# Four element-wise steps of an FFN's tile pair moved from GpSimd to VectorE

## The chip, the cores and the metric

The kernel runs on one core of one Trainium2 chip. The time is the device time of one execution in microseconds; three runs of the kernel before gave 2213.86, 2218.98 and 2221.95 us. An engine is named as in the profile: PE (TensorE), DVE (VectorE), ACT (ScalarE), POOL (GpSimd) and SP (SyncE, which only issues the weight loads here).

## The reference

One inference step of two layers of a decoder, over 512 prompt tokens and 8 x 4 sample tokens, which the kernel keeps side by side as 544 columns. Each layer does

```python
h = h + 0.5 * swiglu(rmsnorm(h, g_ffn1), w1_a, w3_a, w2_a)     # FFN a
h = h + concat(ssd(...), window_attention(...)) @ w_out         # mixing
h = h + 0.5 * swiglu(rmsnorm(h, g_ffn2), w1_b, w3_b, w2_b)     # FFN b
h = h + sigmoid(rmsnorm(h, g_ple) @ w_ple_gate) * (p @ w_ple_proj)

def swiglu(x, w1, w3, w2):
    return (silu(x @ w1) * (x @ w3)) @ w2
```

with a model width of 1024 and an FFN width of 2752, in float32. The change touches the four FFNs (two layers, a and b) alone.

## The kernel before, in words

**Precision.** Every float32 operand of a matmul is split into a high part (a copy rounded to fp32r) and a low part (what is left), and a product is the sum of three: high x high, high x low and low x high. For weights that is `split`: ACT makes the copy (line 100), DVE the difference (line 101). A weight unit is 4 x 128 rows by 128 columns of a weight, 128 x 512 in SBUF. All weight loads are issued by SP, in the order of the program, each into a buffer that an earlier unit must have left.

**An FFN.** The state `h` lies as 8 tiles of 128 x 544. An FFN has a head (`plain`: five plain products against all of `h`, two gated tiles and the remainder of 64 columns, and `block_sums`, which forms four sums of blocks of the normed input) and then 19 *pairs*, in groups of 3, 4, 4, 4 and 4. A pair computes one 128-column tile of x @ w1 and of x @ w3 together, from seven half-products instead of eight, as in Strassen's scheme. With a11, a12 the two halves (in k) of the w1 tile and a21, a22 those of w3, the weight sums are

- q1 = a21 + a22 (line 347, POOL)
- a21 = a21 + a11 (line 348, POOL)
- a11 = a11 + q1 (line 349, DVE)
- a12 = a12 + a11 (line 354, DVE)

each followed by its split; splits of sums are named `q` in the profile (`qh`, `ql`), splits of plain weights `w` (`wh`, `wl`). PE then does seven products of 12 matmuls (line 363) into four PSUM banks, three of which are used twice; after each product DVE reads the bank (lines 373 to 383; the first, line 371, is ACT's) and adds it to `v`, `c2` or `t`, so that a bank's second product waits for the first one's reader. `t` becomes x @ w1 with its columns times Rb (1/rms of the token): the first half in line 379 with the bank's read, the second in line 383 and then line 384 (POOL). `gated` (lines 249 to 254) makes silu: tanh of t/2 on ACT (251), (tanh + 1) * t on DVE (252), times Rb on POOL (253). Line 386 (DVE) multiplies by x @ w3, and `keep` splits the result for the last product (ACT 262, DVE 263).

**Down tiles.** Behind each pair stand two or three of the eight tiles of the last product of the group before (`last(m)`): in group 1, 16 matmuls each, 2, 3 and 3 of them behind its three pairs; in group 2, 18 matmuls each, two behind each pair; in groups 3 to 5, 24 each, two behind each pair. Their matmuls are those of line 128, their split is line 101 again, and DVE adds each half into `h` (line 334). So PE has 84 + 32 or 84 + 48 matmuls per pair in group 1, 120 in group 2, and 132 in groups 3 to 5.

**What sets the order.** The program names tiles and operations; a scheduler with its own cost figures gives each engine its queue, and each engine works through its own in order. A step that is put on another engine can therefore shift other steps on both. Buffers set how far the weights run ahead: six for `raw` (a21, a22 and the down tiles), four for `ra` (a11, a12), two for q1, six for the splits of plain weights and four for those of sums.

Of the kernel before, what the change touches and what calls it, by code (L numbers as in the profile page):

```python
# [12 lines left out]
ALU = mybir.AluOpType  # L13
# [26 lines left out]
def hymba_step(ctx: ExitStack, tc: tile.TileContext, I, O):  # L40
    nc = tc.nc
    V, A, G, PE = nc.vector, nc.scalar, nc.gpsimd, nc.tensor
# [7 lines left out]
    def bank():  # L50
        return psp.tile([128, 512], F32, tag="ps", name="ps")
# [28 lines left out]
    Rb = base.tile([128, N], F32, tag="Rb", name="Rb")  # L80
# [10 lines left out]
    def raw_unit(loads, pool=wp, tag="raw", bufs=None):  # L91
        raw = pool.tile([128, KU, 128], F32, tag=tag, name=tag, bufs=bufs)
        for dst, src in loads:
            nc.sync.dma_start(out=dst(raw), in_=src)
        return raw

    def split(raw, n=KU, pool=wp, tag="w", bufs=None):
        wh = pool.tile([128, KU, 128], F32R, tag=tag + "h", name=tag + "h", bufs=bufs)
        wl = pool.tile([128, KU, 128], F32R, tag=tag + "l", name=tag + "l", bufs=bufs)
        A.copy(wh[:, 0:n, :], raw[:, 0:n, :])  # L100
        V.tensor_sub(wl[:, 0:n, :], raw[:, 0:n, :], wh[:, 0:n, :].bitcast(F32))  # L101
        return wh, wl
# [12 lines left out]
    def terms3(p, k, xh, xl):  # L115
        wh, wl = p[k // KU]
        k %= KU
        return [(wh[:, k, :], xh), (wh[:, k, :], xl), (wl[:, k, :], xh)]
# [20 lines left out]
    HALF = (slice(0, HN), slice(HN, N))  # L139
# [97 lines left out]
    def ffn(g, w1, w3, w2, begun=None):  # L237
# [5 lines left out]
        with tc.tile_pool(name="ffn", bufs=2, reuse_waits="tile") as fp:  # L243
# [5 lines left out]
            def gated(t1, np_=128):  # L249
                th = fp.tile([128, N], F32, tag="th", name="th")  # L250
                A.activation(th[0:np_, :], t1[0:np_, :], AF.Tanh, scale=0.5)
                V.scalar_tensor_tensor(th[0:np_, :], th[0:np_, :], 1.0, t1[0:np_, :], op0=ALU.add, op1=ALU.mult)  # L252
                G.tensor_tensor(th[0:np_, :], th[0:np_, :], Rb[0:np_, :], op=ALU.mult)  # L253
                return th

            def act(ps1, np_=128):
                t1 = fp.tile([128, N], F32, tag="t1", name="t1")
                evac_r(t1, ps1, np_)
                return gated(t1, np_)

            def keep(U, i, u):
                A.copy(U[:, 0, i, :], u)  # L262
                V.tensor_sub(U[:, 1, i, :], u, U[:, 0, i, :].bitcast(F32))
# [73 lines left out]
            def pair(j, sums, U, i):  # L337
                def unit(w, k, pool, tag, bufs):
                    src = w[k * 512:(k + 1) * 512, j * 128:(j + 1) * 128].rearrange("(k p) m -> p k m", p=128)
                    return raw_unit([(lambda t: t, src)], pool, tag, bufs)  # L340

                a11 = unit(w1, 0, fp, "ra", 4)
                a21, a22 = unit(w3, 0, wp, "raw", None), unit(w3, 1, wp, "raw", None)
                a12 = unit(w1, 1, fp, "ra", 4)
                f11 = split(a11)
                q1 = fp.tile([128, KU, 128], F32, tag="q1", name="q1")
                G.tensor_tensor(q1, a21, a22, op=ALU.add)  # L347
                G.tensor_tensor(a21, a21, a11, op=ALU.add)
                V.tensor_tensor(a11, a11, q1, op=ALU.add)
                g2 = split(a11, KU, fp, "q", 4)  # L350
                g3 = split(a21, KU, fp, "q", 4)
                g1 = split(q1, KU, fp, "q", 4)
                f12 = split(a12)
                V.tensor_tensor(a12, a12, a11, op=ALU.add)
                f22 = split(a22)
                g4 = split(a12, KU, fp, "q", 4)
                t2, t3, t1, t4 = sums
                x11, x21, x22 = ((XH[:, k:k + KU, c:c + HN], XL[:, k:k + KU, c:c + HN]) for k, c in ((0, 0), (KU, 0), (KU, HN)))

                def prod(ps, f, x, start):  # L360
                    for k in range(KU):
                        for n, (lhsT, rhs) in enumerate(terms3([f], k, x[0][:, k, :], x[1][:, k, :])):
                            PE.matmul(ps[:, 0:HN], lhsT, rhs, start=start and k == 0 and n == 0, stop=k == KU - 1 and n == 2,  # L363
                                      skip_group_check=not start)

                pa, pb, pc, pd = bank(), bank(), bank(), bank()
                v = fp.tile([128, 2, HN], F32, tag="v", name="v")
                t = fp.tile([128, N], F32, tag="t1", name="t")
                c2 = fp.tile([128, N], F32, tag="c2", name="c2")
                prod(pa, f11, x11, True)  # L370
                A.copy(v[:, 0, :], pa[:, 0:HN])  # L371
                prod(pb, g2, t2, True)
                V.tensor_sub(v[:, 0, :], v[:, 0, :], pb[:, 0:HN])  # L373
                prod(pc, g3, t3, True)
                V.tensor_sub(v[:, 1, :], v[:, 0, :], pc[:, 0:HN])  # L375
                prod(pd, g1, t1, True)
                V.tensor_tensor(c2[:, HALF[1]], v[:, 1, :], pd[:, 0:HN], op=ALU.add)  # L377
                prod(pa, f12, x21, False)
                V.tensor_tensor(t[:, HALF[0]], pa[:, 0:HN], Rb[:, HALF[0]], op=ALU.mult)
                prod(pc, f22, t4, False)  # L380
                V.tensor_sub(c2[:, HALF[0]], v[:, 0, :], pc[:, 0:HN])
                prod(pd, g4, x22, False)
                V.tensor_tensor(t[:, HALF[1]], v[:, 0, :], pd[:, 0:HN], op=ALU.add)  # L383
                G.tensor_tensor(t[:, HALF[1]], t[:, HALF[1]], Rb[:, HALF[1]], op=ALU.mult)  # L384
                th = gated(t)
                V.tensor_tensor(c2, c2, th, op=ALU.mult)  # L386
                keep(U, i, c2)
# [8 lines left out]
            for j0, n in ((2, PH - 1), (5, PH), (9, PH), (13, PH), (17, PH)):  # L396
                U = uset()
                for i in range(n):
                    ms = range(KD * i // n, KD * (i + 1) // n)
                    pair(j0 + i, sums, U, i)  # L400
                    for m in ms:
                        last(m)
                last = lambda m, U=U, j0=j0, n=n: down(j0, n, U, m)
# [884 lines left out]
```

## Time and profile before

| | |
|---|---|
| runs | 2213.86, 2218.98, 2221.95 us (median 2218.98) |
| profiled execution | 2219.62 us, its span 2217.8 us, mean granted clock 0.98 |
| line 347 on POOL | 76 instructions of 128x512, 107.1 us, mean 1409 ns |
| line 348 on POOL | 76 of 128x512, 120.3 us, mean 1583 ns |
| line 384 on POOL | 76 of 128x272, 64.7 us, mean 852 ns |
| line 253 on POOL | 84 of 128x544, 120.9 us, mean 1439 ns, and 4 of 64x544, 8.2 us |
| line 354 on DVE | 76 of 128x512, 95.1 us, mean 1251 ns |
| line 101 on DVE, sums in `ra` | 152 of 128x512, 166.6 us, mean 1096 ns |

Times in the profile are of one execution and in us, unless marked ns. A row such as `L349 TENSOR_TENSOR ra<-ra,q 128x512` is line 349's instruction, out<-in with its shape (partitions x elements). A bracket at the end of a row is the idle time of its engine just before it and what ended that. Rows of one engine can overlap by some tens of ns.

### The profile page before, as it was taken

The numbers are of one execution on the slowest core, as the hardware profiler recorded it, in microseconds if no ns is written. First come the engines' busy times: TensorE is split into PE (matmuls) and PEld (weight loads), VectorE is DVE, ScalarE is ACT, GpSimd is POOL, SyncE is SP. The second block draws the span as 40 slices with busy tenths as digits, with TensorE's granted clock in tenths as the row PEclk, the third lists the DMA queues.
The fourth block names the chain that finished last, engine by engine and source line by source line (L and its number), as shares of the span: only waits on it lengthen the run. The fifth ranks groups of instructions, "written<-read, shape, count | busy, mean of one in ns | idle before, by whom it ended". The sixth has DMA issues, their size and how long they took to land.

```text
span 2217.8 us, 43407 instructions
## 1 busy us (share of the span) xinstructions
PE 2135.3 (96%) x16754; PEld 2088.9 (94%) x16754; DVE 1799.6 (81%) x3250; ACT 953.8 (43%) x1768; POOL 667.4 (30%) x589
## 2 busy tenths in 40 slices
PE   7999999999999999999998999999999998999999
PEld 7989999988899999999988999999898998999998
DVE  7889897589867999886578999874987689998864
ACT  5434443444445344444453344443443453444443
POOL 3323322233522332322123332322334223333220
PEclk9999999999999999999999999999998999999999
DMA  6333332313241433322323333332133423333222
GB/s 178 92 104 91 105 92 76 81 48 89 69 125 47 111 86 105 96 82 84 90 73 102 93 91 101 86 82 70 51 86 87 114 68 92 96 92 105 73 84 72
DMA packets 401210, 197.88 MB, mean 89 GB/s; under 512 B 40270, under 2 KB 400358, under 8 KB 401004
## 3 DMA queue, kind: packets, MB, share of 16 engines
q1 hardware_dynamic: 399420, 194.93, 32.2%
q8 instruction: 132, 2.16, 0.4%
q14 instruction: 74, 0.61, 0.1%
q10 hardware_dynamic: 1584, 0.18, 0.1%
HBM read 187.56 MB, written 9.53 MB: 89 GB/s over the span
## 4 chain that ended last, share of the span: by engine, by line
PE 49%; DVE 10%; issue 3%; ACT 1%; POOL 1%; DMA 1%; SPq 0%; ACTq 0%; DVEq 0%; POOLq 0%
PE ps L128 26%; PE ps L363 20%; DVE wl L101 3%; DVE ql L101 1%; DVE h L334 1%; POOL th L253 1%; DMA raw<-in_w_b 1%; DVE c L386 1%; ACT qh L100 0%; PE ps L910 0%; DVE T L280 0%; ACT U L262 0%; DVE CV L664 0%; DVE v L375 0%; DVE v L373 0%
## 5 line engine op out<-in xcount | busy, mean ns | idle before, releaser
L128 PE MATMUL ps<-U,wh 128*128 128x272 f32 x2752 | 524.8, 289 | 0.0
L100 ACT CAST wh<-raw 128x512 fp32r<-128x512 f32 (+2 forms) x460 | 272.8, 597 | 482.3 <-PE ps L128 255.8
L128 PEld LDWEIGHTS ps<-U,wh 128*128 128x128 f32 x2752 | 433.7, 189 | 0.1
L101 DVE TENSOR_TENSOR wl<-raw,wh 128x512 fp32r<-128x512 f32 (+2 forms) x460 | 345.7, 756 | 84.6 <-ACT wh L100 76.3
L128 PE MATMUL ps<-U,wl 128*128 128x272 f32 x1408 | 400.0, 287 | 0.0
L128 PE MATMUL ps<-XH,wh 128*128 128x272 f32 x1312 | 385.8, 296 | 9.1 <-ACT wk L552 5.3
L128 PE MATMUL ps<-XL,wh 128*128 128x272 f32 x1312 | 380.0, 291 | 1.8 <-DVE XL L158 1.6
L128 PE MATMUL ps<-XH,wl 128*128 128x272 f32 x1280 | 371.4, 291 | 0.0
L128 PEld LDWEIGHTS ps<-U,wl 128*128 128x128 f32 x1408 | 264.3, 188 | 0.0
L128 PEld LDWEIGHTS ps<-XH,wh 128*128 128x128 f32 x1312 | 249.2, 190 | 14.0 <-ACT wk L552 5.7
L128 PEld LDWEIGHTS ps<-XL,wh 128*128 128x128 f32 x1312 | 250.2, 191 | 3.7 <-DVE XL L158 3.3
L128 PEld LDWEIGHTS ps<-XH,wl 128*128 128x128 f32 x1280 | 243.6, 190 | 0.0
L363 PE MATMUL ps<-T,qh 128*128 128x272 f32 x1216 | 236.0, 291 | 4.1 <-DVE T L280 2.9
L384 POOL TENSOR_TENSOR t<-t,Rb 128x272 f32<-128x272 f32 x76 | 64.7, 852 | 475.8 <-DVE t L383 423.8
L347 POOL TENSOR_TENSOR q<-raw 128x512 f32<-128x512 f32 x76 | 107.1, 1409 | 314.2 <-DMA raw<-in_w_b 141.1
L363 PEld LDWEIGHTS ps<-T,qh 128*128 128x128 f32 x1216 | 193.4, 190 | 5.2 <-DVE T L280 3.6
L363 PE MATMUL ps<-XH,wh 128*128 128x272 f32 x608 | 177.6, 292 | 14.5 <-ACT v L371 9.8
L253 POOL TENSOR_TENSOR th<-th,Rb 128x544 f32<-128x544 f32 (+1 forms) x88 | 129.1, 1467 | 179.6 <-DVE th L252 173.5
L363 PE MATMUL ps<-XL,qh 128*128 128x272 f32 x608 | 178.5, 294 | 1.3 <-DVE XL L280 1.3
L363 PE MATMUL ps<-T,ql 128*128 128x272 f32 x608 | 176.9, 292 | 0.9 <-DVE ql L101 0.7
L363 PE MATMUL ps<-XH,qh 128*128 128x272 f32 x608 | 177.1, 291 | 0.6 <-DVE c L377 0.6
L363 PE MATMUL ps<-XH,ql 128*128 128x272 f32 x608 | 177.6, 292 | 0.0
(389 smaller groups left out, 4977.8 us busy)
## 6 DMA issues: line engine op xcount, KB each, us to landing
raw<-in_w_a SPq DMA_DIRECT2D x156, 256.0 KB
raw<-in_w_b SPq DMA_DIRECT2D x156, 256.0 KB
ra<-in_w_a SPq DMA_DIRECT2D x76, 256.0 KB
ra<-in_w_b SPq DMA_DIRECT2D x76, 256.0 KB
raw<-in_w_in SPq DMA_DIRECT2D x60, 256.0 KB
raw<-in_w_ple_gate SPq DMA_DIRECT2D x32, 256.0 KB
raw<-in_w_in SPq DMA_DIRECT2D x32, 128.0 KB
raw<-in_w_out SPq DMA_DIRECT2D x32, 128.0 KB
```

The lines of the kernel that those rows point to most:

```text
L100: A.copy(wh[:, 0:n, :], raw[:, 0:n, :])
L101: V.tensor_sub(wl[:, 0:n, :], raw[:, 0:n, :], wh[:, 0:n, :].bitcast(F32))
L128: PE.matmul(ps[a][:, 0:HN], lhsT, rhs[:, a * HN:(a + 1) * HN], start=gi == 0 and i == 0, stop=gi == n - 1 and i == len(terms) - 1)
L253: G.tensor_tensor(th[0:np_, :], th[0:np_, :], Rb[0:np_, :], op=ALU.mult)
L334: V.scalar_tensor_tensor(h[:, m, HALF[a]], ps[a][:, 0:HN], f, h[:, m, HALF[a]], op0=ALU.mult, op1=ALU.add)
L347: G.tensor_tensor(q1, a21, a22, op=ALU.add)
L363: PE.matmul(ps[:, 0:HN], lhsT, rhs, start=start and k == 0 and n == 0, stop=k == KU - 1 and n == 2, skip_group_check=not start)
L384: G.tensor_tensor(t[:, HALF[1]], t[:, HALF[1]], Rb[:, HALF[1]], op=ALU.mult)
L386: V.tensor_tensor(c2, c2, th, op=ALU.mult)
```

## The change

The four operations of a pair that were POOL's, lines 253, 347, 348 and 384, are given to DVE, operands and results being the same. Line 253 stands in `gated`, so the three gated tiles of the head go with it.

```diff
@@ -250,7 +250,7 @@
                 A.activation(th[0:np_, :], t1[0:np_, :], AF.Tanh, scale=0.5)
                 V.scalar_tensor_tensor(th[0:np_, :], th[0:np_, :], 1.0, t1[0:np_, :], op0=ALU.add, op1=ALU.mult)
-                G.tensor_tensor(th[0:np_, :], th[0:np_, :], Rb[0:np_, :], op=ALU.mult)
+                V.tensor_tensor(th[0:np_, :], th[0:np_, :], Rb[0:np_, :], op=ALU.mult)
                 return th
@@ -344,8 +344,8 @@
                 q1 = fp.tile([128, KU, 128], F32, tag="q1", name="q1")
-                G.tensor_tensor(q1, a21, a22, op=ALU.add)
-                G.tensor_tensor(a21, a21, a11, op=ALU.add)
+                V.tensor_tensor(q1, a21, a22, op=ALU.add)
+                V.tensor_tensor(a21, a21, a11, op=ALU.add)
                 V.tensor_tensor(a11, a11, q1, op=ALU.add)
@@ -381,7 +381,7 @@
                 V.tensor_tensor(t[:, HALF[1]], v[:, 0, :], pd[:, 0:HN], op=ALU.add)
-                G.tensor_tensor(t[:, HALF[1]], t[:, HALF[1]], Rb[:, HALF[1]], op=ALU.mult)
+                V.tensor_tensor(t[:, HALF[1]], t[:, HALF[1]], Rb[:, HALF[1]], op=ALU.mult)
                 th = gated(t)
                 V.tensor_tensor(c2, c2, th, op=ALU.mult)
```

The queues of DVE are in another order by it. In group 2, DVE's queue of the kernel before, around the first evacuations of one pair (`v_9764`); `ra_9922`, `ra_9928`, `raw_9924` and `q1_9934` belong to the next pair's weights, `ra_9725` is the pair's own a12:

```order
L263 TENSOR_TENSOR U_9312<-c2_9563,U_9312 128x544
L334 SCALAR_TENSOR_TENSOR h_70<-ps_9698,h_70 128x272
L101 TENSOR_TENSOR wl_9931<-ra_9922,wh_9930 128x512
L349 TENSOR_TENSOR ra_9922<-ra_9922,q1_9934 128x512
L101 TENSOR_TENSOR wl_9951<-ra_9928,wh_9950 128x512
L373 TENSOR_TENSOR v_9764<-v_9764,ps_9761 128x272
L354 TENSOR_TENSOR ra_9928<-ra_9928,ra_9922 128x512
L101 TENSOR_TENSOR ql_9939<-ra_9922,qh_9938 128x512
L375 TENSOR_TENSOR v_9764<-v_9764,ps_9762 128x272
```

and the same place after the change:

```order
L263 TENSOR_TENSOR U_9312<-c2_9563,U_9312 128x544
L354 TENSOR_TENSOR ra_9725<-ra_9725,ra_9719 128x512
L101 TENSOR_TENSOR wl_9897<-raw_9894,wh_9896 128x384
L373 TENSOR_TENSOR v_9764<-v_9764,ps_9761 128x272
L101 TENSOR_TENSOR ql_9757<-ra_9725,qh_9756 128x512
L101 TENSOR_TENSOR wl_9931<-ra_9922,wh_9930 128x512
L375 TENSOR_TENSOR v_9764<-v_9764,ps_9762 128x272
L347 TENSOR_TENSOR q1_9934<-raw_9924,raw_9926 128x512
L377 TENSOR_TENSOR c2_9766<-v_9764,ps_9763 128x272
L348 TENSOR_TENSOR raw_9924<-raw_9924,ra_9922 128x512
```

The next pair's first sums now stand behind L375 of this pair instead of ahead of it, and the last sum of this pair's own weights (L354 on `ra_9725`) and its split have moved in between its evacuations.

In a pair of groups 3 to 5, DVE's queue before, from one pair's L386 on (`v_11032` is the next pair, `wl_11171` a split of a down tile):

```order
L386 TENSOR_TENSOR c2_10818<-c2_10818,th_10911 128x544
L334 SCALAR_TENSOR_TENSOR h_70<-ps_10925,h_70 128x272
L101 TENSOR_TENSOR wl_11171<-raw_11168,wh_11170 128x512
L263 TENSOR_TENSOR U_10125<-c2_10818,U_10125 128x544
L334 SCALAR_TENSOR_TENSOR h_70<-ps_10958,h_70 128x272
L334 SCALAR_TENSOR_TENSOR h_70<-ps_10959,h_70 128x272
L101 TENSOR_TENSOR wl_11211<-ra_11202,wh_11210 128x512
L349 TENSOR_TENSOR ra_11202<-ra_11202,q1_11214 128x512
L101 TENSOR_TENSOR wl_11231<-ra_11208,wh_11230 128x512
L354 TENSOR_TENSOR ra_11208<-ra_11208,ra_11202 128x512
L373 TENSOR_TENSOR v_11032<-v_11032,ps_11029 128x272
L101 TENSOR_TENSOR ql_11219<-ra_11202,qh_11218 128x512
```

and after the change:

```order
L386 TENSOR_TENSOR c2_10818<-c2_10818,th_10911 128x544
L334 SCALAR_TENSOR_TENSOR h_70<-ps_10958,h_70 128x272
L101 TENSOR_TENSOR wl_11171<-raw_11168,wh_11170 128x512
L263 TENSOR_TENSOR U_10125<-c2_10818,U_10125 128x544
L334 SCALAR_TENSOR_TENSOR h_70<-ps_10959,h_70 128x272
L101 TENSOR_TENSOR wl_11211<-ra_11202,wh_11210 128x512
L349 TENSOR_TENSOR ra_11202<-ra_11202,q1_11214 128x512
L101 TENSOR_TENSOR wl_11231<-ra_11208,wh_11230 128x512
L347 TENSOR_TENSOR q1_11429<-raw_11419,raw_11421 128x512
L373 TENSOR_TENSOR v_11032<-v_11032,ps_11029 128x272
L101 TENSOR_TENSOR ql_11219<-ra_11202,qh_11218 128x512
L354 TENSOR_TENSOR ra_11208<-ra_11208,ra_11202 128x512
```

The sum L347 of a later pair (`q1_11429`) now stands in DVE's queue ahead of L373 and the evacuations behind it, five instructions behind the split `wl_11171`, whose end frees the buffer that the last of L347's two loads goes into.

## The prediction

> **What bounds the kernel now.** I read the busy line first, then the windows, the chain of waits, the starts of one instruction that every pair has (line 386), and last the rows of one pair on VectorE and GpSimd.
>
> ```profile
> PE 2135.3 (96%) x16754; PEld 2088.9 (94%) x16754; DVE 1799.6 (81%) x3250; ACT 953.8 (43%) x1768; POOL 667.4 (30%) x589
> ```
>
> TensorE (PE) is busy for 2135.3 of the span's 2217.8 us, so at most 82.5 us can be had without touching matmuls. VectorE (DVE) at 81% looks like the last engine to give more work. That is an average; by stages it reads otherwise (columns: window, length, busy of PE, weight load, DVE, ACT, POOL, then the granted clock):
>
> ```profile
> 1180.00:1285.00 105.00, 94.31 (x719) 92.78 (x718) 97.82 (x153) 40.84 (x76) 35.05 (x26) 0.97 0.34 95
> 1285.00:1468.00 183.00, 183.00 (x1459) 183.00 (x1459) 158.04 (x261) 77.14 (x129) 51.24 (x40) 1.00 0.33 92
> 1212.00:1220.00 8.00, 5.47 (x24) 5.48 (x25) 5.89 (x11) 0.97 (x2) 1.57 (x1) 0.57 0.32 87
> ```
>
> These lie in the third FFN. In the pair groups 3 to 5 (second row) PE never rests and DVE has 25 us free. In groups 1 and 2 (first row) PE rests 10.7 us of 105, and DVE is busy for 93%. PE waits there for DVE:
>
> ```profile
> PE ps L363 <- DVE v L375: 29.9, 21, 4.3
> 1214.53 0.82 PE L363 MATMUL ps<-T,wh 128*128 128x272 f32 x2 [4.34 <-DVE v L375]
> ```
>
> A product that writes a bank which L375 must first read stands still. After the longest such stall the clock row shows 0.57: 24 matmuls take 5.47 us, 0.228 each, against the full rate in the chain of waits:
>
> ```profile
> 834.78 6.01 PE ps L128 x48
> 840.78 10.57 PE ps L363 x84
> ```
>
> That is 0.1255 us per matmul. From one L386 to the next, PE has 84 matmuls of products and the down tiles of the pair between. In group 1 these are 116, 132 and 132 matmuls up to the first pair of group 2; in group 2 four times 120 (two down tiles of 18). At full rate, group 1 needs 380 x 0.1255 = 47.7 us and group 2 480 x 0.1255 = 60.2 us per FFN. The starts of the 1st, 4th and 8th pair's L386, for the four FFNs:
>
> ```profile
> 73.65 0.72 DVE L386 TENSOR_TENSOR c<-c,th 128x544 f32<-128x544 f32 x1 [0.77 <-POOL th L253]
> 127.92 0.72 DVE L386 TENSOR_TENSOR c<-c,th 128x544 f32<-128x544 f32 x1 [1.26 <-POOL th L253]
> 194.52 0.73 DVE L386 TENSOR_TENSOR c<-c,th 128x544 f32<-128x544 f32 x1 [1.14 <-POOL th L253]
> 719.03 0.72 DVE L386 TENSOR_TENSOR c<-c,th 128x544 f32<-128x544 f32 x1 [0.78 <-POOL th L253]
> 774.28 0.71 DVE L386 TENSOR_TENSOR c<-c,th 128x544 f32<-128x544 f32 x1
> 839.05 0.73 DVE L386 TENSOR_TENSOR c<-c,th 128x544 f32<-128x544 f32 x1 [1.14 <-POOL th L253]
> 1167.96 0.73 DVE L386 TENSOR_TENSOR c<-c,th 128x544 f32<-128x544 f32 x1 [0.78 <-POOL th L253]
> 1224.87 0.71 DVE L386 TENSOR_TENSOR c<-c,th 128x544 f32<-128x544 f32 x1
> 1289.65 0.73 DVE L386 TENSOR_TENSOR c<-c,th 128x544 f32<-128x544 f32 x1 [1.14 <-POOL th L253]
> 1814.00 0.72 DVE L386 TENSOR_TENSOR c<-c,th 128x544 f32<-128x544 f32 x1 [0.78 <-POOL th L253]
> 1870.72 0.71 DVE L386 TENSOR_TENSOR c<-c,th 128x544 f32<-128x544 f32 x1
> 1935.51 0.73 DVE L386 TENSOR_TENSOR c<-c,th 128x544 f32<-128x544 f32 x1 [1.14 <-POOL th L253]
> ```
>
> Group 1 takes 54.3, 55.3, 56.9 and 56.7 us: 32.4 us over PE's need in all. Group 2 takes 66.6, 64.8, 64.8 and 64.8: 20.0 us over. So 52 of the 82.5 us lie where DVE sets the pace, and the pair groups 3 to 5 have nothing to give.
>
> **Why DVE is slow there.** One pair of group 2, on DVE and then on POOL (start, duration):
>
> ```profile
> 789.28 1.58 DVE L101 TENSOR_TENSOR wl<-raw,wh 128x384 fp32r<-128x384 f32 x1
> 790.78 0.71 DVE L386 TENSOR_TENSOR c<-c,th 128x544 f32<-128x544 f32 x1
> 791.42 0.43 DVE L334 SCALAR_TENSOR_TENSOR h<-ps,h 128x272 f32<-128x272 f32 x1
> ...
> 793.92 1.78 DVE L349 TENSOR_TENSOR ra<-ra,q 128x512 f32<-128x512 f32 x1
> 795.63 1.79 DVE L101 TENSOR_TENSOR wl<-ra,wh 128x512 fp32r<-128x512 f32 x1
> 797.34 0.43 DVE L373 TENSOR_TENSOR v<-v,ps 128x272 f32<-128x272 f32 x1
> 797.69 0.68 DVE L354 TENSOR_TENSOR ra<-ra 128x512 f32<-128x512 f32 x1
> 798.29 0.68 DVE L101 TENSOR_TENSOR ql<-ra,qh 128x512 fp32r<-128x512 f32 x1
> 798.89 0.42 DVE L375 TENSOR_TENSOR v<-v,ps 128x272 f32<-128x272 f32 x1
> 799.24 0.68 DVE L101 TENSOR_TENSOR ql<-raw,qh 128x512 fp32r<-128x512 f32 x1
> ...
> 803.26 1.27 DVE L101 TENSOR_TENSOR ql<-ra,qh 128x512 fp32r<-128x512 f32 x1
> ```
>
> ```profile
> 789.08 1.36 POOL L253 TENSOR_TENSOR th<-th,Rb 128x544 f32<-128x544 f32 x1 [1.61 <-DVE th L252]
> 793.87 1.29 POOL L347 TENSOR_TENSOR q<-raw 128x512 f32<-128x512 f32 x1 [3.42 <-DMA raw<-in_w_b]
> 795.23 1.63 POOL L348 TENSOR_TENSOR raw<-raw,ra 128x512 f32<-128x512 f32 x1
> 803.21 0.78 POOL L384 TENSOR_TENSOR t<-t,Rb 128x272 f32<-128x272 f32 x1 [6.35 <-DVE t L383]
> ```
>
> Each of the four GpSimd instructions falls on a DVE instruction with two operands in SBUF, and that one ends 0.4 to 0.6 us after GpSimd's does: 1.58, 1.78, 1.79 and 1.27 us, where the same forms undisturbed take about 0.55 (estimated from 128x512's 0.68), 0.68, 0.68 and 0.68. So one pair pays 1.0 + 1.1 + 1.1 + 0.6 = 3.8 us on DVE for GpSimd's help.
>
> **The change, part by part.** All four operations become DVE instructions. Start to start (rows overlap by some 0.07 us) a 128x512 costs 0.60 (797.69 to 798.29), a 128x272 0.35 (798.89 to 799.24) and a 128x544 0.64 (790.78 to 791.42). L347 and L348 add 1.20, L384 0.35, L253 0.64: 2.19 us per pair, 76 pairs, and 12 more L253 in the four heads. GpSimd then has no work left in a pair, so the 3.8 us should go: a net 1.6 us less on DVE per pair, in the groups where DVE is the bound.
>
> *Group 2.* A pair takes (66.6 + 3 x 64.8) / 16 = 16.31 us now. 16.31 - 3.8 + 2.19 = 14.7, plus about 0.3 because L252, L253 and L386 now follow each other on one engine with a result in between: 15.0, against PE's 15.06. DVE falls just under PE. With the two so close I leave 0.2 us per pair: gain 20.0 - 16 x 0.2, about 17. Least: the gap between the two rows closes only half (10). Most: 20.
>
> *Group 1.* The same net gain per pair, on intervals of 18.1 to 19 us. By DVE's work alone they would fall to PE's need. But the first pairs have no stock: their weights are prepared by DVE while it still finishes the block sums, and the longest stall (4.34 us, with the half clock behind it) lies here. I keep some 2.5 us per FFN: gain 32.4 - 10, about 22. Least 0, most 32.
>
> *Groups 3 to 5.* DVE is busy 158.04 of 183 us, or 14.3 of a pair's 132 x 0.1255 = 16.57. With 2.19 more and no relief at all that is 16.5, still under PE; with relief near 14. I cost them at nothing. PE's own matmuls hide it. The cover is thin only if DVE must wait (first rival).
>
> *Waits on POOL, and the heads.*
>
> ```profile
> DVE c L386 <- POOL th L253: 64.8, 58, 1.8
> DVE u L292 <- POOL th L253: 8.3, 7, 1.3
> ```
>
> The 64.8 us of waits at L386 go too, but most lie in groups 3 to 5 and are worth nothing. In the heads 8.3 us of DVE waits at L292 stand ahead of the block sums that PE's first pair needs; I take half, 4 (0 to 8).
>
> Sum: 17 + 22 + 4 = 43 us off the profiled run's 2219.62 (span 2217.8 and 1.8 around it; 0.6 above the median of the runs): **2177 us**, 1.9% less. The ends of the terms give 10 to 60 us, so 2160 to 2210.
>
> **The rivals.**
>
> *A: only half comes back.* The scheduler has put DVE's queue in a new order in groups 1 and 2: weight splits that ran a pair ahead now stand among the evacuations of the pair before. If L375 stands as late as it does now in group 1, the 32.4 us stay and only group 2's 17 is had: about 2202. For it: group 1's stalls depend on order, not only on sums.
>
> *B: nothing.* The saved 3.8 us reappear as the added 2.19 us and as waits inside the longer DVE chain L383, L384, (tanh on ACT), L252, L253, L386: 2217. Against it: the rows above show the overlap four times in one pair.
>
> *C, slower: L347 holds DVE's queue.* On POOL this sum waited for its weights with nothing behind it but L348. On DVE the evacuations that PE needs (L373, L375) stand behind it. The rows of a pair in group 3:
>
> ```profile
> 922.88 0.68 DVE L101 TENSOR_TENSOR wl<-raw,wh 128x512 fp32r<-128x512 f32 x1
> 923.59 0.37 SPq L94 DMA_DIRECT2D raw<-in_w_b  x1
> 926.54 1.43 POOL L347 TENSOR_TENSOR q<-raw 128x512 f32<-128x512 f32 x1 [4.69 <-DMA raw<-in_w_b]
> ```
>
> A split frees the buffer, the load is issued, and 2.95 us later L347 starts. In the new order five DVE instructions (0.64 + 0.35 + 0.60 + 0.60 + 0.60 = 2.8 us) stand between that split and L347, so DVE waits some 0.2 us, inside the 16.57 - 14.3 = 2.3 us (some 1.5 when its small gaps are counted) that a pair leaves. If the load came x us late, the 48 pairs of groups 3 to 5 would each lose x - 1.5: it eats the whole gain at x = 2.4, and a load taking twice as long (x = 3) gives 2177 + 72 = 2249.
>
> *D, slower: the long rows are not GpSimd's doing.* If the 1.6 us rows stayed long without GpSimd, each pair of groups 1 and 2 would just get 2.19 us more: 28 x 2.19 = 61, so 2281. The rows speak against it: the four long ones are those, and only those, that run under a GpSimd row, and each ends just after it. The Trainium skill, Perfetto Trace Analysis, section Optimizing Scalar/DVE Operations, says that when VectorE is saturated, giving some of its work to ScalarE or even GpSimd may make sense, which for groups 1 and 2 is this rival; it adds that VectorE and GpSimd share an SBUF read port, so that moving work between those two might not help. By its first half the sum would be 2281, by its second it stays at 2177; the rows of this pair agree with the second (1.78 us against 0.68).
>
> **How the numbers follow.** Forecast 0.62, A 0.20, B 0.08, C 0.07, D 0.03. A measurement of this kernel can tell about 0.5% from no change, here 11 us: faster means under 2208, slower over 2230. The forecast and A lie below: 0.82. B with the low edge of C gives 0.09 within, C and D 0.09 slower. Range: the lower end is the 60 us bound less 2 (2158); the upper takes A whole and stops at 2208, leaving B, C, D outside. The likeliest case's own range is 2160 to 2192.
>
> **What would show it.** Right: POOL has no row of these four lines left; L101, L349 and L354 fall to 0.68 everywhere; the L386 starts in group 2 lie 15.1 to 15.4 us apart, in group 1 within 3 us per FFN of 47.7; PE's wait on L375 falls below 10 us. Wrong in group 1: these rows shrink, yet PE still waits for L375 with the low clock behind it. Wrong by C: DVE's idle time before L347 behind a DMA, and L386 intervals over 16.6 in groups 3 to 5.

## The result and the profile after

The changed kernel takes 2154.53 us (median of 2149.38 to 2156.97) against 2218.49 us for the kernel before, measured beside it. The ratio is 0.9715, with a 95% interval from 0.9696 to 0.9734: 64 us less, where 42 were forecast (2177 us) and 2158 us was the low end of the range. The profiled execution took 2153.38 us, its span 2151.6.

The page's busy line of the changed kernel, and two of its windows, the four pairs of group 2 and ten pairs of groups 3 to 5 in the second FFN:

```profile
PE 2112.0 (98%) x16754; PEld 2071.7 (96%) x16754; DVE 1803.1 (84%) x3566; ACT 953.4 (44%) x1768; POOL 247.3 (11%) x273
732.35:792.61 60.26, 60.26 (x482) 60.26 (x481) 58.95 (x117) 27.15 (x49) 0.00 (x0) 1.00 0.41 113
809.18:974.91 165.73, 165.73 (x1322) 165.73 (x1321) 151.37 (x282) 72.02 (x121) 0.00 (x0) 1.00 0.33 91
```

The same group 2 in the kernel before:

```profile
754.21:823.18 68.97, 62.85 (x482) 61.98 (x481) 66.06 (x102) 27.42 (x51) 22.56 (x17) 0.98 0.35 97
```

Three things stand in these rows. VectorE has 316 instructions more and is busy for 1803.1 us against 1799.6: what it was given, it no longer spends standing still. TensorE now never rests in group 2 (60.26 of 60.26 us, and 480 matmuls x 0.1255 are 60.24), and VectorE does its larger share with 58.95 us of busy time instead of 66.06. (Of the 8.71 us by which this stretch is shorter, 7.11 are VectorE's busy time and 1.60 its idle time.) And TensorE's own busy time fell by 23.3 us with the same 16754 matmuls, while the mean granted clock rose from 0.98 to 0.989: a matmul at the low clock counts as busy for longer (0.228 us against 0.1255 in the prediction's rows).

VectorE's groups of the changed kernel (line, form, count, busy us, mean ns, then its idle time before them), and the group in which GpSimd is now busy longest, which was fourth before, behind lines 253, 348 and 347:

```profile
L101 DVE TENSOR_TENSOR ql<-ra,qh 128x512 fp32r<-128x512 f32 x152 | 104.3, 686 | 5.3 <-ACT qh L100 0.4
L253 DVE TENSOR_TENSOR th<-th,Rb 128x544 f32<-128x544 f32 x84 | 60.6, 721 | 1.4
L347 DVE TENSOR_TENSOR q<-raw 128x512 f32<-128x512 f32 x76 | 52.3, 688 | 6.1 <-DMA raw<-in_w_a 4.6 <-DMA raw<-in_w_b 0.9
L384 DVE TENSOR_TENSOR t<-t,Rb 128x272 f32<-128x272 f32 x76 | 33.1, 435 | 0.2
L354 DVE TENSOR_TENSOR ra<-ra 128x512 f32<-128x512 f32 x76 | 52.0, 684 | 0.1
```

```profile
L167 POOL TENSOR_TENSOR acc<-acc,sq 128x544 f32<-128x544 f32 x49 | 68.1, 1389 | 1496.5 <-ACT sq L166 1496.3
```

The splits `ql<-ra` fell from a mean of 1096 ns to 686, L354 from 1251 to 684. L347 waits 5.5 us for its loads in the whole program.

To see where the time went, the start of each pair's first product on TensorE serves better than the starts of L386 that the prediction used, because L386 itself lay behind GpSimd. Between these starts TensorE has the same number of matmuls in both kernels. The two measures cut the time at other places: the products of pair 4 belong to group 2 here, but to "group 1" between the 1st and the 4th L386. The table is worked out from them, in us against the profiled kernel before, summed over the four FFNs ("rest" is all from the last pair of one FFN to the first of the next, with the program's two ends, which moves by up to 6 us from kernel to kernel):

```
                          rest   pairs 1-3   pairs 4-7   pair 8    pairs 9-18   all
                                 (group 1)   (group 2)   (first of groups 3-5)
changed kernel            -1.5     -22.1       -39.1      -3.5        0.0     -66.2
```

### The profile page after: what moved, and what is told of

Its sections match the earlier page's. It is cut to its first block, busy times and chain, and to the rows that moved or that the text cites. A ratio compares the mean times of both kernels' runs of the same rounds, so it can differ in the third digit from the quotient of the medians.

```text
span 2151.6 us, 43014 instructions
## 1 busy us (share of the span) xinstructions
PE 2112.0 (98%) x16754; PEld 2071.7 (96%) x16754; DVE 1803.1 (84%) x3566; ACT 953.4 (44%) x1768; POOL 247.3 (11%) x273
## 4 chain that ended last, share of the span: by engine, by line
PE 88%; DVE 8%; ACT 2%; DMA 1%; issue 1%; SPq 0%; POOL 0%; ACTq 0%; DVEq 0%
PE ps L128 45%; PE ps L363 36%; DVE wl L101 1%; PE ps L910 1%; ACT Y L269 1%; DVE CV L664 1%; DVE T L280 1%; DMA raw<-in_w_a 1%; PE ps L558 1%; DVE wk L527 0%; PE ps L551 0%; PE ps L522 0%; DVE ql L101 0%; DVE XL L158 0%; PE ps L432 0%
## 5 line engine op out<-in xcount | busy, mean ns | idle before, releaser
L101 DVE TENSOR_TENSOR wl<-raw,wh 128x512 fp32r<-128x512 f32 (+2 forms) x460 | 317.9, 695 | 87.9 <-ACT wh L100 67.3
L128 PE MATMUL ps<-XH,wl 128*128 128x272 f32 x1280 | 371.4, 291 | 0.0
L167 POOL TENSOR_TENSOR acc<-acc,sq 128x544 f32<-128x544 f32 x49 | 68.1, 1389 | 1496.5 <-ACT sq L166 1496.3
L334 DVE SCALAR_TENSOR_TENSOR h<-ps,h 128x272 f32<-128x272 f32 x384 | 166.4, 435 | 27.6 <-PE ps L128 27.0
L363 PE MATMUL ps<-XH,wl 128*128 128x272 f32 x608 | 175.3, 288 | 0.0
```

What stands on the lines that cost most here:

```text
L128: PE.matmul(ps[a][:, 0:HN], lhsT, rhs[:, a * HN:(a + 1) * HN], start=gi == 0 and i == 0, stop=gi == n - 1 and i == len(terms) - 1)
L167: add.tensor_tensor(self.acc, self.acc, sq, op=ALU.add)
L334: V.scalar_tensor_tensor(h[:, m, HALF[a]], ps[a][:, 0:HN], f, h[:, m, HALF[a]], op0=ALU.mult, op1=ALU.add)
```

## The experiments

**GpSimd's reads put back.** The changed kernel, with four GpSimd instructions per pair on tiles that are dead by then.

```diff
-                g1 = split(q1, KU, fp, "q", 4)
+                g1 = split(q1, KU, fp, "q", 4); G.tensor_tensor(q1, q1, Rb[:, 0:512]..., op=ALU.mult); G.tensor_tensor(q1, q1, Rb[:, 0:512]..., op=ALU.mult)
...
-                V.tensor_tensor(c2, c2, th, op=ALU.mult)
+                V.tensor_tensor(c2, c2, th, op=ALU.mult); G.tensor_tensor(t[:, HALF[1]], t[:, HALF[1]], Rb[:, HALF[1]], op=ALU.mult); G.tensor_tensor(th, th, Rb, op=ALU.mult)
```

> The changed kernel, with GpSimd given four two-operand instructions per pair again, of the old shapes, on tiles that nobody reads any more (q1 times Rb twice behind q1's split, the half of t and th times Rb behind line 386). The result is the same, and the order of the instructions on VectorE, TensorE, ScalarE and SyncE is the changed kernel's, instruction for instruction. Theory L (the time was lost because a VectorE instruction with two SBUF operands stands still while GpSimd reads SBUF): VectorE has its 2.19 us per pair and up to 3.8 us of standing still, so groups 1 and 2 are slower than even before (28 pairs x 2.19 = 61 us over 2219) and groups 3 to 5, at 14.3 + 2.19 of 16.57 plus small gaps, turn VectorE-bound too: 2240 to 2310 us. Theory O (the time was won by the new order of VectorE's queue): 2150 to 2165. Theory W (it was won because VectorE and TensorE no longer wait for results of slow GpSimd instructions): nobody waits for these results, so 2150 to 2165 too.

Measured: 2312.7 us, ratio 1.0428 (1.0412 to 1.0443). Against the changed kernel that is 158 us for instructions whose results nobody reads, with VectorE's, TensorE's, ScalarE's and SyncE's queues unchanged. First GpSimd's rows in a pair of groups 3 to 5, then VectorE's rows there:

```profile
899.23 3.00 POOL L352 TENSOR_TENSOR q<-q,Rb 128x512 f32<-128x512 f32 x2 [7.12 <-DVE ql L101]
905.66 1.30 POOL L386 TENSOR_TENSOR t<-t,Rb 128x272 f32<-128x272 f32 x1 [3.44 <-DVE th L252]
907.63 1.38 POOL L386 TENSOR_TENSOR th<-th,Rb 128x544 f32<-128x544 f32 x1 [0.67 <-DVE c L386]
```

```profile
899.43 1.64 DVE L101 TENSOR_TENSOR wl<-raw,wh 128x512 fp32r<-128x512 f32 x1
900.99 0.42 DVE L381 TENSOR_TENSOR c<-v,ps 128x272 f32<-128x272 f32 x1
901.34 1.43 DVE L101 TENSOR_TENSOR wl<-raw,wh 128x512 fp32r<-128x512 f32 x1
...
907.83 1.73 DVE L101 TENSOR_TENSOR wl<-raw,wh 128x512 fp32r<-128x512 f32 x1
```

and VectorE's group of these splits in the whole program:

```profile
L101 DVE TENSOR_TENSOR wl<-raw,wh 128x512 fp32r<-128x512 f32 x380 | 401.5, 1060 | 74.8 <-ACT wh L100 64.8 <-DMA raw<-in_w_in 2.9
```

The splits beside GpSimd's reads take 1.4 to 1.7 us again; L381 between them, whose second operand is in PSUM, takes its 0.42. The mean of the group is 1060 ns. By the pairs' starts, groups 3 to 5 lose 81 us against the kernel before (10.2 and 71.0), group 2 1.2 and group 1 11.8. So neither the new order (theory O) nor the end of the waits (theory W) can be the main cause: with the same order, and with nobody who reads GpSimd's results, the kernel is slower than the one before. No wait of a pair's line on VectorE for GpSimd stands in this run's list of waits either, so it isn't a late release of the tiles. TensorE, on its side, waits for VectorE's L375 for 96.7 us, 64 times, where it was 29.9 us before.

**GpSimd's writes alone.** The same tiles at the same places, filled with zeros.

```diff
-                g1 = split(q1, KU, fp, "q", 4)
+                g1 = split(q1, KU, fp, "q", 4); G.memset(q1, 0.0); G.memset(q1, 0.0)
...
-                V.tensor_tensor(c2, c2, th, op=ALU.mult)
+                V.tensor_tensor(c2, c2, th, op=ALU.mult); G.memset(t[:, HALF[1]], 0.0); G.memset(th, 0.0)
```

> As the run with four dead instructions on GpSimd, the same tiles at the same places, but GpSimd fills them with zeros, which writes SBUF and reads nothing. Order on the other engines unchanged, result the same. Theory L in the form that GpSimd's reads do the harm: 2150 to 2165, and VectorE rows of 0.68 us stay so beside the fills. If any GpSimd access stops VectorE: as slow as the run with reads. Theories O and W: 2150 to 2165. If it is slow though the rows beside the fills stay short, it is the later release of q1, t and th that costs, and the run with reads must be read with that taken off.

Measured: 2154.34 us, ratio 0.9716 (0.9696 to 0.9735), the changed kernel's time. A fill is shorter than a multiplication, so the total time alone doesn't settle it. GpSimd's group and a fill, then the same group of VectorE's splits (mean 728 ns) and the row beside that fill:

```profile
L352 POOL MEMSET q<- 128x512 f32 x152 | 80.2, 527 | 567.7 <-DVE ql L101 502.7 <-issue 60.6
777.48 1.11 POOL L352 MEMSET q<- 128x512 f32 x2 [9.22 <-DVE ql L101]
```

```profile
L101 DVE TENSOR_TENSOR wl<-raw,wh 128x512 fp32r<-128x512 f32 x380 | 275.7, 728 | 87.8 <-ACT wh L100 69.7 <-DMA raw<-in_w_in 2.9 <-PE ps L172 0.2
778.04 0.68 DVE L354 TENSOR_TENSOR ra<-ra 128x512 f32<-128x512 f32 x1
```

The fills come to 147 us of GpSimd (80.2, and 42.3 and 24.8 for the fills of th and t), about a third of the multiplications' 432 (242.4, 108.5 and 80.8). If any access did the harm, a third of 158, some 50 us by this estimate, would show; nothing does, and L354 takes 0.68 us beside a fill. The later release of the tiles costs nothing either, as far as the fills hold them. The Trainium skill, SBUF — State Buffer, section Who interferes with whom, says that a VectorE instruction with two SBUF inputs contends with a GpSimd instruction that reads SBUF and not with one that only writes it; these two runs agree, 2312.7 us with reads and 2154.34 with writes.

**One dead read instead of four.** Only the first of the multiplications of q1.

```diff
-                g1 = split(q1, KU, fp, "q", 4)
+                g1 = split(q1, KU, fp, "q", 4); G.tensor_tensor(q1, q1, Rb[:, 0:512]..., op=ALU.mult)
```

> The changed kernel with one dead GpSimd instruction per pair instead of four (q1 times Rb, 128x512, behind q1's split); result and order on the other engines unchanged. Theory L with a threshold: one such instruction holds VectorE for about 1.1 us. In groups 3 to 5 VectorE is busy for 151 of 166 us, 1.4 us free per pair, so they stay at TensorE's 16.57; in group 2 it is busy for 98% of 60.3 us, so nearly all of 1.1 us per pair shows: 16 x 0.8 to 1.1, and about half of that in group 1's twelve: 2165 to 2180. If the cost were spread over all pairs alike: 76 x 1.1 = 84, 2235 to 2240.

Measured: 2164.35 us, ratio 0.9768 (0.9748 to 0.9788), just under what was expected, and the loss is at another place. Group 2 keeps TensorE's pace (60.26 us); the 10 us show in the first three pairs (13 us won against the kernel before, where the changed kernel wins 22) and in groups 3 to 5 (3.4). Nearly all of the 3.4 us fall on one pair of group 3 in each of the later three FFNs. VectorE prepares weights ahead, so a lag in group 2 may be paid there, but that was not tried; busy time in a window did not say how much could be added. That the cost is far from 76 x 1.1 = 84 us did hold. In group 2, GpSimd and then VectorE:

```profile
772.21 2.69 POOL L352 TENSOR_TENSOR q<-q,Rb 128x512 f32<-128x512 f32 x1 [12.95 <-DVE ql L101]
```

```profile
772.59 0.69 DVE L354 TENSOR_TENSOR ra<-ra 128x512 f32<-128x512 f32 x1
773.20 0.55 DVE L101 TENSOR_TENSOR wl<-raw,wh 128x384 fp32r<-128x384 f32 x1
773.67 0.43 DVE L373 TENSOR_TENSOR v<-v,ps 128x272 f32<-128x272 f32 x1
774.02 1.42 DVE L101 TENSOR_TENSOR ql<-ra,qh 128x512 fp32r<-128x512 f32 x1
```

Here GpSimd seems to be the one held first: its instruction takes 2.69 us, where those of groups 3 to 5 mostly take 1.3; two-operand rows of VectorE beside its first part keep their 0.69 and 0.55, and the split that meets its end pays 1.42.

**The two halves of the change.** First the weight sums alone, then tanh's part and the half tile alone.

```diff
-                G.tensor_tensor(q1, a21, a22, op=ALU.add)
-                G.tensor_tensor(a21, a21, a11, op=ALU.add)
+                V.tensor_tensor(q1, a21, a22, op=ALU.add)
+                V.tensor_tensor(a21, a21, a11, op=ALU.add)
```

> From the kernel before, only lines 347 and 348 (the two weight sums) on VectorE. Theory L: per pair 1.1 + 1.1 us of standing still go and 1.2 us of work comes, 1.0 net of the full change's 1.6; of the 56 us in groups 1 and 2 some 35 to 45 are won, the heads' 9 us mostly not: 2172 to 2190. Theory W with the sums as the late result (L349 waits for q1): nearly all, 2155 to 2165. Theory W with tanh's part as the late result: nothing, 2210 to 2220.

Measured: 2212.53 us, ratio 0.9985 (0.9969 to 1.0): nearly nothing, where 2172 to 2190 was expected.

```diff
-                G.tensor_tensor(th[0:np_, :], th[0:np_, :], Rb[0:np_, :], op=ALU.mult)
+                V.tensor_tensor(th[0:np_, :], th[0:np_, :], Rb[0:np_, :], op=ALU.mult)
...
-                G.tensor_tensor(t[:, HALF[1]], t[:, HALF[1]], Rb[:, HALF[1]], op=ALU.mult)
+                V.tensor_tensor(t[:, HALF[1]], t[:, HALF[1]], Rb[:, HALF[1]], op=ALU.mult)
```

> From the kernel before, only lines 253 and 384 (tanh part and half a tile times 1/rms) on VectorE; the weight sums stay on GpSimd. Theory L: per pair 1.0 + 0.6 us go and 0.99 come, 0.6 net: 15 to 25 us in groups 1 and 2, and up to 9 in the heads: 2185 to 2205. Theory W with tanh's part as the late result: nearly all, 2155 to 2165. With the sums as the late result: 2210 to 2220.

Measured: 2178.4 us, ratio 0.9816 (0.9793 to 0.984): 40 us, more than expected. The pairs' starts say where (us against the profiled kernel before):

```
                            rest   group 1   group 2   pair 8   pairs 9-18    all
sums alone (347, 348)        1.0    -14.2     -19.4     -0.5      30.2       -2.9
tanh's part, half tile       4.1    -17.7     -22.6     -2.0       0.0      -38.2
```

The sums alone do win 34 us in groups 1 and 2, as the theory of the blocked operand has it, and lose 30 in groups 3 to 5, where a pair mostly takes 17.1 to 17.7 us instead of 16.57. Three rows of one such pair on VectorE, and its waits in the whole program:

```profile
898.37 0.73 DVE L252 SCALAR_TENSOR_TENSOR th<-th,t 128x544 f32<-128x544 f32 x1 [1.35 <-ACT th L251]
900.57 0.72 DVE L386 TENSOR_TENSOR c<-c,th 128x544 f32<-128x544 f32 x1 [1.12 <-POOL th L253]
905.24 0.69 DVE L347 TENSOR_TENSOR q<-raw 128x512 f32<-128x512 f32 x1 [1.06 <-DMA raw<-in_w_b]
```

```profile
DVE th L252 <- ACT th L251: 87.1, 79, 1.6
DVE c L386 <- POOL th L253: 65.9, 63, 1.1
DVE q L347 <- DMA raw<-in_w_a: 28.8, 26, 3.3
DVE q L347 <- DMA raw<-in_w_b: 25.1, 27, 2.2
```

VectorE has work for less than its pair and still is late, and it stops three times for 3.5 us together: twice behind the steps that stayed on GpSimd (L252 waits for ACT's tanh, which waits for L384), once behind a load. The wait of the prediction's rival C, a queue held by L347, is here 54 us, against 5.5 in the full change.

**All but one line.** The change without line 384, and without line 253.

```diff
-                G.tensor_tensor(t[:, HALF[1]], t[:, HALF[1]], Rb[:, HALF[1]], op=ALU.mult)
+                V.tensor_tensor(t[:, HALF[1]], t[:, HALF[1]], Rb[:, HALF[1]], op=ALU.mult)
```

The line above is left as it was before in the first of them, and line 253 in the second.

> The change without line 384: the sums and line 253 on VectorE, half a tile times 1/rms on GpSimd. With the sums alone moved, the pairs of groups 3 to 5 took 17.3 us instead of 16.57, and VectorE stood idle in each at three places: 1.35 us at L252 (tanh, behind GpSimd's L384), 1.12 us at L386 (behind GpSimd's L253), 1.06 us at L347 (its load). Theory Q (a step left on GpSimd in the middle of a pair's last chain stops VectorE's queue, and the sums have used up the slack that hid this): L386's wait goes for 0.64 us of work, 17.3 - 1.1 + 0.6 = 16.8, so groups 3 to 5 lose 10 us instead of 30, and groups 1 and 2 win a little more: 2175 to 2195. Theory D (it is the load behind L347 alone that stops the queue): groups 3 to 5 stay at 17.3 or more, 2205 to 2220.

Measured: 2153.51 us, ratio 0.9714 (0.9693 to 0.9735), as fast as the full change.

> The change without line 253: the sums and line 384 on VectorE, tanh's part times 1/rms on GpSimd. Theory Q: the wait at L252 falls from 1.35 to about 0.65 (ACT's tanh alone) for 0.35 us of work, the 1.1 us at L386 stay: 17.3 - 0.7 + 0.35 = 16.95 in groups 3 to 5, that is 18 us lost there instead of 30: 2185 to 2205. Theory D: 2205 to 2220.

Measured: 2170.15 us, ratio 0.9789 (0.9772 to 0.9807). VectorE's waits, first without 384, then without 253:

```profile
DVE th L252 <- ACT th L251: 79.5, 82, 1.6
DVE q L347 <- DMA raw<-in_w_a: 12.9, 25, 3.0
DVE q L347 <- DMA raw<-in_w_b: 6.4, 22, 0.4
```

```profile
DVE c L386 <- POOL th L253: 69.1, 65, 1.5
DVE th L252 <- ACT th L251: 25.9, 58, 0.7
DVE q L347 <- DMA raw<-in_w_a: 14.8, 23, 3.7
DVE q L347 <- DMA raw<-in_w_b: 6.8, 21, 0.4
```

In both kernels nearly all pairs of groups 3 to 5 run at 16.57 again, though one keeps nearly the whole wait at L252 and the other the whole wait at L386. So neither of these waits alone turns the pairs VectorE-bound. But in both the wait at L347 fell as well, from 54 us to 19 and 22, since the scheduler put L347 one place further back. These runs therefore don't tell whether the load or the sum of the three stops cost the sums-alone kernel its 30 us; that stays open.

**Line 253 alone.**

```diff
-                G.tensor_tensor(th[0:np_, :], th[0:np_, :], Rb[0:np_, :], op=ALU.mult)
+                V.tensor_tensor(th[0:np_, :], th[0:np_, :], Rb[0:np_, :], op=ALU.mult)
```

> From the kernel before, line 253 alone on VectorE. While GpSimd does L253, VectorE either stands still beside it (1.0 us in group 2) or waits for it at L386 (1.1 us); 0.64 us of work comes instead. The full change without line 384 was as fast as the full change, and lines 253 and 384 together won 40 us. So line 253 alone should win most of these 40: 2178 to 2195. If it is line 384 that mattered beside the sums: 2205 to 2220.

Measured: 2181.25 us, ratio 0.9835 (0.9813 to 0.9856): 35 us, over half of the gain, from one line. By the pairs' starts group 1 wins 16.8 us, group 2 18.1.

**By groups.** The four lines on VectorE only in the heads and groups 1 and 2 (`E = V if j < 9 else G`, and V in `plain`), then only in groups 3 to 5.

```diff
+                E = V if j < 9 else G
...
-                G.tensor_tensor(q1, a21, a22, op=ALU.add)
+                E.tensor_tensor(q1, a21, a22, op=ALU.add)
```

> The four lines on VectorE in the heads and the pair groups 1 and 2 only; in groups 3 to 5 they stay on GpSimd as before. If the whole gain sits where VectorE set the pace, this kernel has nearly all of it: 2152 to 2160 (the 3.5 us of each group 3's first pair may be missing). If groups 3 to 5 had a share of their own that the starts of the pairs hide: above 2165.

Measured: 2166.57 us, ratio 0.9772 (0.9757 to 0.9786). Groups 1 and 2 have all of the gain (22.3 and 39.1 us), as expected. The missing 12 us lie in the first pair of group 3, where the steps change engines: it takes 19.1 to 20.7 us instead of 16.57, with TensorE waiting for L375 (8.2 us, 6 times, in the whole program). Why the change-over costs that was not tried.

> The complement: the four lines on VectorE in groups 3 to 5 only. Theory L with TensorE as the bound there: 2213 to 2220, the same as before. If moving the steps costs those groups something that the full change hides: above 2225.

Measured: 2207.42 us, ratio 0.9956 (0.9942 to 0.9971), 9 us faster where no difference was expected. Groups 3 to 5 won nothing, but the last pairs of group 2 did (10.3 us in all). The weights of group 3's first pair are prepared there, and their sums were VectorE's now; that this is the reason was not tried apart.

**More of the same.** The changed kernel, with the seven large element-wise steps of the mixing stage on VectorE too, and with the sums of squares of the norms there.

```diff
-                G.tensor_tensor(P2[:, :, k0:256], P2[:, :, k0:256], bc(dn, 2, nk), op=ALU.mult)
+                V.tensor_tensor(P2[:, :, k0:256], P2[:, :, k0:256], bc(dn, 2, nk), op=ALU.mult)
```

This is line 545; lines 770, 787, 792, 813, 895 and 906 likewise.

> The changed kernel with the seven large element-wise steps of the mixing stage that GpSimd still has (lines 545, 770, 787, 792, 813, 895, 906) on VectorE too. In the mixing stage of the changed kernel TensorE is idle for some 8 us per layer, waits for ScalarE's copies behind these steps among it, and VectorE is busy for 75%. Theory L: a few us may be won: 2145 to 2155. If VectorE's longer queue delays what TensorE needs there: 2155 to 2170.

Measured: 2152.61 us, ratio 0.9709 (0.9691 to 0.9727).

```diff
-                    self.square(c, V if c == KD - 1 else G)
+                    self.square(c, V)
```

The call at line 1208 is changed likewise.

> The changed kernel with the sums of squares of the norms (line 167, 49 instructions of 128x544, 68 us on GpSimd) on VectorE too. They run under the last down tiles of an FFN and at the stages' starts, where TensorE does not wait for VectorE: 2150 to 2157, no difference from the changed kernel that can be measured. If VectorE's standing still beside them delayed the heads: up to 5 us less.

Measured: 2157.57 us, ratio 0.9729 (0.9713 to 0.9746). Both intervals overlap the changed kernel's, so neither is a better version: TensorE is busy for 98% of the span, and little is left outside it.

## Why the prediction was right or wrong

*The mechanism was right.* The rows that ran beside GpSimd's instructions were long because of them, and they fell to 0.68 us. Putting reads back and writes back, in the same order of instructions, shows that it is the reading. The whole trace says the same: in the kernel before, 206 rows of 128x512 of lines 101, 349 and 354 took over 0.9 us, 168 us in all above 0.684 each. Every one of them overlaps a two-operand row of GpSimd and ends 0.55 us after one (0.545 to 0.556). In the changed kernel 15 such rows are left, beside what GpSimd still has to do.

*TensorE's need between two L386.* The prediction took 380 matmuls for group 1 and 480 for group 2. L386 lies behind TensorE by an amount that differs from pair to pair, so the number is another: in the last three FFNs 370 matmuls start in the first interval before the change and 369 after, and 477 and 484 in the second (in the first FFN 389 and 372, 455 and 485). Group 1's need is thus some 46.4 us there, not 47.7, and its interval could fall, and fell, below what the prediction held to be the least.

*Group 2: right, in part by luck.* 17 us were forecast; by the prediction's own measure, L386 of the 4th to the 8th pair, it is 17.7 (66.60 to 60.89 in the first FFN, 64.77 to 60.77 and the same in the others). The sum 16.31 - 3.8 + 2.19 = 14.7 us of VectorE per pair is what the window shows, 58.95 / 4 = 14.7. The 0.3 us for the longer chain and the 0.2 us left for the close race were not needed: TensorE does not rest there at all, and the interval is over 60.2 us because more than 480 matmuls lie in it.

*Group 1: the term was mis-sized, and this is the step that failed.* 22 us were forecast, at most 32; 34.9 came (54.27, 55.25, 56.91 and 56.72 us fell to 48.56, 46.54, 46.56 and 46.55). The step is "I keep some 2.5 us per FFN" for the missing stock of weights. One of its grounds was the longest stall, 4.34 us at 1214.53. It does lie between the 1st and the 4th L386, but in pair 4, the first of group 2, as the start of that pair's first product shows (kernel before):

```profile
1202.46 0.29 PE L363 MATMUL ps<-XH,wh 128*128 128x272 f32 x1
```

All but 0.5 of the 29.9 us that TensorE waited for L375 fell on pairs 4 to 8. With VectorE's shorter rows they went whole: the wait no longer stands in the list. So they were VectorE's pace, which the change lifts, and not a cost of the start that it leaves. What VectorE's work on the block sums and the first weights costs shows in pair 1, ahead of the first L386 and so outside this term, and it is still there in part. The changed kernel in the second FFN, where the first L386 starts at 700.93, first in pair 1, then from the run of pair 2's products to the first product of pair 4:

```profile
692.50 0.36 PE L363 MATMUL ps<-XH,wh 128*128 128x272 f32 x1 [1.53 <-DVE v L373]
699.23:732.35 33.12, 33.12 (x264) 33.00 (x263) 32.58 (x66) 14.10 (x26) 0.00 (x0) 1.00 0.37 102
```

With VectorE quick again, TensorE does not rest in that stretch in the later three FFNs (33.12 to 33.14 us), and only the first FFN needs 2.6 us more. Rival A, in which group 1's stalls stay, did not happen, and neither did rival B, in which nothing is won.

*The heads: mis-sized.* 4 us were forecast, at most 8. Up to the first L386 of an FFN, 9.0 us went, and all of it between the start of pair 1's first product and that L386 (20.92, 22.58, 22.61 and 22.45 us fell to 18.89, 19.99, 20.09 and 20.10). The term counted the waits at L292 ahead of the block sums. TensorE's waits for these sums are indeed gone; in the kernel before they were

```profile
PE ps L363 <- DVE T L280: 2.9, 3, 1.0
PE ps L363 <- DVE XL L280: 1.3, 3, 0.4
```

Left out was that the first L386 itself waited for L253, 0.77 or 0.78 us in each FFN. How the rest divides was not taken apart.

*Groups 3 to 5: nothing, and 5.2 us by the same measure.* By TensorE's starts the pairs 9 to 18 did not change by 0.1 us. The first pair of group 3 lost its excess of 0.87 us per FFN (3.5 in all), still VectorE's lag from group 2, and L386 itself moved forward by its lost wait.

*The range.* Its low end was the sum of the terms' upper ends, 20 + 32 + 8 = 60 us with nothing for groups 3 to 5, and three of the four were no bounds: 34.9 us came where 32 was the most, 9.0 where 8 was, and 5.2 where nothing was. The 52.4 us over TensorE's need were measured between instructions that lay behind GpSimd, so what was lost ahead of the first of them and behind the last was not in it. Nor is "at most 82.5 us" a bound, since it took TensorE's busy time as fixed, and 23.3 us of that went too, with the stalls and the low clock behind them. The median moved by 64 us.

*Rival C* was costed at a wait of 0.2 us per pair; it is 5.5 us in the whole program. *Rival D* is refuted by the result, in which the rows are short, and by the run with reads: 158 us for four instructions per pair that GpSimd does beside VectorE's own. The first half of the sentence weighed there (the Trainium skill, Perfetto Trace Analysis, section Optimizing Scalar/DVE Operations: give a saturated VectorE's work to others) does not hold for these steps, and its second half (the shared port may make it useless between these two) is milder than what was measured, 64 us won by taking the work back.

## What to carry to other kernels

When rows of one VectorE form have two lengths, lay GpSimd's rows beside them: here every 128x512 row of lines 101, 349 and 354 over 0.9 us ended 0.55 us after a two-operand GpSimd row. GpSimd's help may cost VectorE more than the work it takes away (3.8 us against 2.19 per pair here). Try the steps of a pair together and not only one by one: the sums alone gave 6 us of the 64, line 253 alone 35, and all but line 384 the whole. And for the most that a change can bring, measure between starts on the engine that bounds the program, count the matmuls that lie between them in the trace, and count slow-clock time as part of what can be had.

## What had not been expected of the hardware

GpSimd's rows grow as well: a 128x512 multiplication, mostly 1.3 us in groups 3 to 5, took 2.69 us beside VectorE's row of two-operand instructions, and with the sums on VectorE the mean of GpSimd's L384 rose from 852 to 1206 ns. GpSimd's fill of 128x512 takes 0.53 us, against 1.4 to 1.6 for its two-operand instruction of that size, and costs VectorE nothing that these runs can measure.
